# Final rows of the first 128 tokens moved from VectorE to ScalarE and accumulating transfers, and VectorE's last operations written in a fixed order

## The chip, the core and the metric

The program runs on one NeuronCore of a Trainium2 chip. Its engines are TensorE (PE in the rows, its weight load PEld), VectorE (DVE), ScalarE (ACT), GpSimd (POOL) and SyncE (SP); SP, ACT and POOL can issue transfers, which 16 DMA engines carry out. The metric is the device time of one execution in microseconds, lower being better.

## What is computed

One decoder layer in fp32 for 512 tokens of width 2048. An input projection feeds differential attention, a Mamba-2 mixer and cross-attention; their gated outputs are put side by side (`mixed`, 512 x 2048) and go through the output projection, a norm and the residual. Only the end matters here:

```python
def rms_norm(x, w):
    y = x * lax.rsqrt(jnp.mean(x * x, axis=-1, keepdims=True) + NORM_EPS)
    return y * w
...
    mixed = jnp.concatenate([diff_out, ssd_out, xattn_out], axis=-1)
    return x + rms_norm(mixed @ w_out, post_norm_w)
```

The norm needs the sum of squares over all 2048 columns of a token before any of its columns can be written.

## The kernel before

**Output projection.** `mixed @ w_out` is made in four groups `g` of 512 columns. In each, seven block products `q` of 256 columns take the place of eight, and their sums give the result. A product has four units `u`, and each number is split into a high and a low part, so each small product is three matmuls of 128x256 (lines 99 to 101). The sums are gathered in SBUF tiles `oacc{g}{c}`: 128 tokens by `t` (2) by `r` (2) by 256 columns, `c` being the half of the 512 tokens. A "row" `t` in the code below is one block of 128 tokens: rows 0 and 1 lie in `c` = 0, rows 2 and 3 in `c` = 1.

**The tail.** In the last group the products 5 and 3 touch only `c` = 1, and they are made last, for row 2 (PSUM tiles `oq35`, `oq33`) and then for row 3 (`oq35b`, `oq33b`). Rows 0 and 1 are complete before. For each row, in `write_rows`:

1. ScalarE has squared the sums (`finish`, line 1066; tile `jk`, results in `ssq`), VectorE has multiplied them by the norm's weight and by -0.5 or 0.5 (line 1070).
2. VectorE adds the eight partial sums of `ssq` (line 1082), ScalarE takes the logarithm and the exponential (lines 291, 292), and VectorE sharpens the root in three tiny operations (lines 293 to 295). The result `ors` is -2 times the reciprocal root.
3. VectorE makes `xr = oacc * ors + xr` for four pieces of 512 columns (line 1088). `xr{t}{h}` is the row of `x`, loaded in two halves of 512 KB by SP (line 1078) into eight buffers that the weights of the projection leave free.
4. SP stores the row in two halves (line 1096); row 3 goes in four pieces of 256 KB, alternately by SP and ScalarE's queue (line 1093).

**Order.** A scheduler with a timeline of its own orders the instructions of each engine. `tc.keep_in_program_order(op)` fixes one to its place in the text, and `tc.issue_after(x)` keeps what is inside behind `x`. In before, nothing that VectorE does in the tail is fixed. POOL issues the accumulating loads of weights (line 968, pieces `oA`, 512 KB each in runs of 1 KB), the last of them at 851.28 us, and has nothing after it.

Of the kernel before, what the change touches and what calls it, by code (L numbers as in the profile page):

```python
# [15 lines left out]
AF = mybir.ActivationFunctionType  # L16
ALU = mybir.AluOpType
AX = mybir.AxisListType
PSUM = bass.MemoryType.PSUM

P = 128
# [3 lines left out]
NT = S // P  # L25
M = 256
EPS = 1e-6
# [42 lines left out]
def hymba_kernel(ctx: ExitStack, tc: tile.TileContext, x, mem, positions, pre_norm_w, w_in,  # L70
# [3 lines left out]
    nc = tc.nc  # L74
    x2, mem2, out2 = x[0], mem[0], out[0]
# [4 lines left out]
    small = ctx.enter_context(tc.tile_pool(name="small", bufs=4))  # L80
# [5 lines left out]
    def bank(tag, name):  # L86
        if tag == "d":
            return psd.tile([P, 512], F32, tag="d", name=name)
        return pss.tile([P, 512], F32, tag=tag, name=name, bufs=SIDE[tag])

    def ft(pool, shape, tag, name, bufs=None, dt=F32):
        kw = {} if bufs is None else {"bufs": bufs}
        return pool.tile(shape, dt, tag=tag, name=name, **kw)
# [54 lines left out]
    epsc = const.tile([P, 1], F32, name="epsc")  # L148
# [140 lines left out]
    def neg2_rstd(y, t, v):  # L289

        nc.scalar.activation(t, v, AF.Ln, bias=epsc)
        nc.scalar.activation(y, t, AF.Exp, scale=-0.5)
        nc.vector.tensor_tensor(t, y, y, ALU.mult)
        nc.vector.scalar_tensor_tensor(t, v, EPS, t, ALU.add, ALU.mult)
        nc.vector.scalar_tensor_tensor(y, t, 3.0, y, ALU.subtract, ALU.mult)
# [3 lines left out]
    def push(name, side="right"):  # L299
        cm = tc.tile_pool(name=name, bufs=1, side=side, reuse_waits="tile")  # L300
        open_pools.append(cm)
        return cm.__enter__()
# [7 lines left out]
    def slot(n, name, dt=F32):  # L310

        if n % 2 == 0:
            slot_pairs[n // 2] = slots_p.tile([P, 2, S], dt, tag=f"s{n // 2}", name=name)
        return slot_pairs[n // 2][:, n % 2]
# [63 lines left out]
    ps = dense_xs(memT, [bank("d", f"mv{t}") for t in range(2)], 512)  # L378
# [17 lines left out]
    for t in range(NT):  # L396
        rs = row_rstd(x_rows[t], f"x{t}")
# [12 lines left out]
    for h in range(4):  # L410
        ps = dense_ws(memT, M, f"mk{h}")
# [29 lines left out]
    ps = dense_xs(hT, [bank("dddt"[t].replace("t", "tr"), f"v0_{t}") for t in range(NT)], 264)  # L441
# [37 lines left out]
    for c in range(2):  # L479
        for i in range(2):  # L480
            h = 2 * c + i
            ps = dense_ws(hT, S, f"xq{h}")
# [6 lines left out]
            for qp in range(2):  # L489
# [11 lines left out]
                for j in range(2):  # L501
                    nc.scalar.activation(pt[:, j], sc[:, j * M:(j + 1) * M], AF.Exp,
                                         bias=nm[:, j:j + 1], scale=XSC, accum_out=ls[:, j:j + 1])
# [16 lines left out]
            o = slot(12 + h, f"xo{h}")  # L520
# [123 lines left out]
    for g in range(2):  # L644
        for i in range(2):
            ps = dense_ws(hT, S, f"z{g}{i}")
# [15 lines left out]
        rt = ft(sp, [P, S], "rt", f"rt{g}", 1)  # L662
# [47 lines left out]
    for t in range(NT):  # L710
        for b in range(4):
            src = slice(32 * t, 32 * t + 32)
            dst = slice(32 * b, 32 * b + 32)
            ts = slice(t * P, (t + 1) * P)
# [18 lines left out]
    for c in range(2):  # L733
        for i in range(2):
            ps = dense_ws(hT, S, f"xg{c}{i}")
# [163 lines left out]
    for p in range(4):  # L899
        if p:  # L900
            vb = [bank("d", f"v{p}_{t}") for t in range(2)]
            ps = dense_xs(hT, [vb[t // 2][:, t % 2 * 256:t % 2 * 256 + 256] for t in range(NT)],
                          256, share=2)
            v_pair[p] = evac_v(ps, str(p))
        q = [rope(dense_ws(hT, S, f"q{2 * p + i}"), "q", 2 * p + i) for i in range(2)]
        k = [rope(dense_ws(hT, S, f"k{2 * p + i}"), "k", 2 * p + i) for i in range(2)]
# [20 lines left out]
    op = push("op")  # L927
# [13 lines left out]
    ssq = const.tile([P, NT, 8], F32, name="ssq")  # L941
# [4 lines left out]
    NG = D // 512  # L946
# [106 lines left out]
    oacc = {}  # L1053

    def acc(g, r, c):

        if (g, c) not in oacc:
            oacc[g, c] = slots_p.tile([P, 2, 2, 256], F32, tag=f"s{2 * g + c}",
                                      name=f"oacc{g}{c}")
        return oacc[g, c][:, :, r]  # L1060

    def finish(g, r, c, ts=(0, 1)):
        o = acc(g, r, c)
        jk = ft(ep, [P, 256], "jk", f"jk{g}{r}{c}{ts[0]}", 2, BF16)
        for t in ts:
            nc.scalar.activation(jk, o[:, t], AF.Square, scale=1.0 / math.sqrt(D),
                                 accum_out=ssq[:, 2 * c + t, 2 * g + r:2 * g + r + 1])
        w = pws[g][:, r].unsqueeze(1).broadcast_to([P, len(ts), 256])
        tt = slice(ts[0], ts[-1] + 1)
        nc.vector.scalar_tensor_tensor(o[:, tt], o[:, tt], (-0.5, 0.5)[r], w, ALU.mult,  # L1070
                                       ALU.mult)

    xr = {}

    def load_rows(t):
        for h in range(2):
            xr[t, h] = raw_tile(f"xr{t}{h}")
            nc.sync.dma_start(xr[t, h], x2[t * P:(t + 1) * P, h * 1024:(h + 1) * 1024])

    def write_rows(t):  # L1080
        ss = ft(small, [P, 1], "ss", f"oss{t}")
        nc.vector.tensor_reduce(ss, ssq[:, t], AX.X, ALU.add)
        y = ft(small, [P, 1], "rs", f"ors{t}")
        tt = ft(small, [P, 1], "rt", f"ort{t}")
        neg2_rstd(y, tt, ss)
        for g in range(NG):
            xs = xr[t, g // 2][:, (g % 2) * 512:(g % 2) * 512 + 512]
            nc.vector.scalar_tensor_tensor(
                xs, oacc[g, t // 2][:, t % 2].rearrange("p r c -> p (r c)"), y, xs,
                ALU.mult, ALU.add)  # L1090
            q = nc.scalar if t == NT - 1 and g % 2 else nc.sync
            if t == NT - 1:
                q.dma_start(out2[t * P:(t + 1) * P, 512 * g:512 * g + 512],
                            xr[t, g // 2][:, (g % 2) * 512:(g % 2) * 512 + 512])
            elif g % 2:
                q.dma_start(out2[t * P:(t + 1) * P, 512 * g - 512:512 * g + 512], xr[t, g // 2])

    def product(n, ps, ts=(0, 1)):
        hi, lo = split[n]
        g, q, u = seq[n]  # L1100
        for t in ts:
            tsl = slice(t * P, (t + 1) * P)
            for kk in range(2):
                bh, bl = comb[2 * u + kk][PROD[q][1]]
                last = mm3(ps[:, t], bh[:, tsl], bl[:, tsl], hi[kk], lo[kk],
                    u == 0 and kk == 0 and t == ts[0], u == 3 and kk == 1 and t == ts[-1])
        return last
# [28 lines left out]
    qps, qps2 = {}, {}  # L1136
    for n, (g, q, u) in enumerate(seq):
# [13 lines left out]
        ps = qps[g, q]  # L1151
        if n < len(seq) - 8:
            last = product(n, ps)
# [4 lines left out]
        T = lambda o, x, y: V.tensor_tensor(o, x, y, ALU.add)  # L1158
# [14 lines left out]
        if q == 3:  # L1173
# [2 lines left out]
            T(acc(g, 0, 1), acc(g, 0, 1), ps)  # L1176
            finish(g, 1, 1)
            finish(g, 0, 1)
    for t in (0, 1):
        load_rows(t)  # L1180
        write_rows(t)
    g = NG - 1
    N = len(seq)
    for t in (0, 1):
        load_rows(2 + t)
        for q, n in ((5, N - 8), (3, N - 4)):
            ps = qps2[q] if t else qps[g, q]
            with tc.issue_after(last.ins):
              for u in range(4):
                last = product(n + u, ps, (t,))  # L1190
            for r in range(2):
                if q == 5 or r == 0:
                    T(acc(g, r, 1)[:, t], acc(g, r, 1)[:, t], ps[:, t])
            finish(g, int(q == 5), 1, (t,))
        write_rows(2 + t)
    while open_pools:
        pop()

# [32 lines left out]
```

## Time and profile before

| | us |
|---|---|
| median of three runs | 904.86 |
| those runs | 901.61, 904.86, 905.66 |
| the profiled execution, its time | 903.45 |
| its span, first to last instruction | 901.7 |
| last matmul on the chain of waits starts | 890.72 |
| last operation of VectorE ends | 898.24 |

Times in the rows count from the span's start. The profiled execution is 1.75 us longer than its span, and lies 1.41 us under the median of the three runs, inside their spread.

### The profile page before, as it was taken

What the parts mean: (1) busy time and instruction counts of PE and PEld (TensorE: products, weight loads), DVE (VectorE), ACT (ScalarE), POOL (GpSimd) and SP (SyncE); (2) the same over time, 40 slices, a digit from 0 to 9 for tenths busy, and PEclk for the clock granted to TensorE, in tenths of its full rate; (3) what the DMA queues carried; (4) which work ended last, traced back from release to release, by engine and by line L of the source; (5) the groups of instructions that cost most, each with busy time, mean ns of one, the idle gap of its engine ahead of it and who ended that gap; (6) DMA issues with size and microseconds to landing.
All of it is one profiled execution on the core that took longest, in us unless ns stands there. A gap on an engine that the chain in (4) does not pass through costs nothing.

```text
span 901.7 us, 13703 instructions
## 1 busy us (share of the span) xinstructions
PE 882.7 (98%) x5187; PEld 773.9 (86%) x5187; DVE 607.6 (67%) x1150; ACT 467.9 (52%) x823; POOL 131.2 (15%) x139
## 2 busy tenths in 40 slices
PE   8999999999999999999999999999999999999995
PEld 6899888888888888898889889888888888999995
DVE  5775545595565542485768578676877689877797
ACT  4754234455356643344455445456676675564562
POOL 3310000006000212330230123023100011110200
PEclk9999999999999999999999999999999999999998
DMA  9862322354343333433342433334232475785946
GB/s 307 302 166 71 94 71 71 102 143 115 95 130 81 94 94 93 116 98 92 95 117 71 106 95 82 94 97 115 71 94 74 126 191 120 181 195 119 214 131 245
DMA packets 150205, 111.86 MB, mean 124 GB/s; under 512 B 8869, under 2 KB 139634, under 8 KB 150138
## 3 DMA queue, kind: packets, MB, share of 16 engines
q1 hardware_dynamic: 141434, 102.58, 40.1%
q0 software_dynamic: 8416, 7.87, 5.7%
q8 instruction: 41, 0.67, 0.3%
q10 hardware_dynamic: 288, 0.52, 0.2%
q14 instruction: 26, 0.21, 0.1%
HBM read 102.02 MB, written 4.21 MB: 118 GB/s over the span
## 4 chain that ended last, share of the span: by engine, by line
PE 87%; DVE 4%; DMA 4%; issue 3%; ACT 1%; POOL 0%; SPq 0%; DVEq 0%; POOLq 0%; ACTq 0%
PE v L101 3%; PE v L99 3%; PE v L100 3%; PE q L99 3%; PE q L100 3%; PE k L100 3%; PE k L99 3%; PE q L101 3%; PE xbc L99 3%; PE k L101 3%; PE xbc L101 3%; PE xbc L100 3%; PE oq L100 3%; PE dg L101 3%; PE dg L100 3%; DMA oA<-in_w_out_dram 3%
## 5 line engine op out<-in xcount | busy, mean ns | idle before, releaser
L104 DVE TENSOR_TENSOR wlo<-raw,whi 128x1024 fp32r<-128x1024 f32 (+2 forms) x121 | 152.1, 1257 | 119.4 <-ACT whi L247 105.8
L247 ACT ACTIVATE whi<-raw 128x1024 fp32r<-128x1024 f32 (+1 forms) x104 | 110.2, 1060 | 127.4 <-issue 36.7
L1048 ACT ACTIVATE owh<-oA 128x512 fp32r<-128x512 f32 x106 | 65.8, 630 | 59.2 <-PE oq L101 46.1
L104 DVE TENSOR_TENSOR owl<-oA,owh 128x512 fp32r<-128x512 f32 x106 | 71.6, 690 | 16.5 <-ACT owh L1048 16.1
L100 PE MATMUL v<-wlo,hT 128*128 128x256 f32 (+1 forms) x256 | 72.9, 285 | 0.0
L101 PE MATMUL v<-whi,hT 128*128 128x256 f32 (+1 forms) x256 | 72.6, 285 | 0.0
L99 PE MATMUL v<-whi,hT 128*128 128x256 f32 (+1 forms) x256 | 72.4, 285 | 0.0
L803 ACT ACTIVATE p<-sc,nm 128x128 f32<-128x128 f32 (+3 forms) x64 | 33.4, 525 | 60.0 <-DVE nm L799 52.8
L100 PE MATMUL k<-hT,whi 128*128 128x512 f32 x128 | 51.0, 398 | 0.0
L101 PE MATMUL xbc<-hT,wlo 128*128 128x512 f32 x128 | 50.8, 397 | 0.0
L100 PE MATMUL dg<-hT,whi 128*128 128x512 f32 x128 | 50.7, 396 | 0.0
L101 PE MATMUL dg<-hT,wlo 128*128 128x512 f32 x128 | 50.7, 396 | 0.0
L99 PE MATMUL q<-hT,whi 128*128 128x512 f32 x128 | 50.7, 396 | 0.0
L100 PE MATMUL xbc<-hT,whi 128*128 128x512 f32 x128 | 50.6, 395 | 0.0
L99 PE MATMUL dg<-hT,whi 128*128 128x512 f32 x128 | 50.5, 395 | 0.0
L101 PE MATMUL k<-hT,wlo 128*128 128x512 f32 x128 | 50.5, 395 | 0.0
L100 PE MATMUL q<-hT,whi 128*128 128x512 f32 x128 | 50.4, 394 | 0.0
L99 PE MATMUL k<-hT,whi 128*128 128x512 f32 x128 | 50.4, 394 | 0.0
L99 PE MATMUL xbc<-hT,whi 128*128 128x512 f32 x128 | 50.4, 394 | 0.0
L101 PE MATMUL q<-hT,wlo 128*128 128x512 f32 x128 | 50.3, 393 | 0.0
L100 PEld LDWEIGHTS v<-wlo,hT 128*128 128x128 f32 x256 | 48.5, 189 | 0.3
L99 PEld LDWEIGHTS v<-whi,hT 128*128 128x128 f32 x256 | 48.3, 189 | 0.3
(445 smaller groups left out, 2569.0 us busy)
## 6 DMA issues: line engine op xcount, KB each, us to landing
raw<-in_w_in_dram SPq DMA_DIRECT2D x104, 512.0 KB, 3.9
oA<-in_w_out_dram SPq DMA_DIRECT2D x32, 512.0 KB, 5.5
raw<-in_w_mem_kv_dram SPq DMA_DIRECT2D x15, 512.0 KB, 5.4
oA<-in_w_out_dram POOLq DMA_DIRECT2D x14, 512.0 KB, 6.9
x_rows<-in_x_dram SPq DMA_DIRECT2D x8, 512.0 KB, 8.8
xr<-in_x_dram SPq DMA_DIRECT2D x8, 512.0 KB, 7.9
out_dram<-xr SPq DMA_DIRECT2D x6, 512.0 KB, 2.7
mem_rows<-in_mem_dram SPq DMA_DIRECT2D x8, 256.0 KB, 5.8
```

The costliest lines, as they stand in the source:

```text
L99: nc.tensor.matmul(ps, ah, bh, start=start, stop=False)
L100: nc.tensor.matmul(ps, ah, bl, start=False, stop=False)
L101: return nc.tensor.matmul(ps, al, bh, start=False, stop=stop)
L104: nc.vector.tensor_tensor(lo, src, hi.bitcast(F32), ALU.subtract)
L247: nc.scalar.activation(hi[:, :n], raw[:, :n], AF.Copy)
L803: nc.scalar.activation(pc[c][:, :w], sc[c][:, :w], AF.Exp, bias=nm[:, c:c + 1], scale=DSC, accum_out=ls[:, c:c + 1])
L1048: nc.scalar.activation(hi, src, AF.Copy)
```

## The change

For row 0, VectorE's four operations of step 3 are gone. ScalarE multiplies the sums by `ors` in place (line 1209, four copies of 128x512 with a scale), and POOL's queue adds each result onto `xr` in SBUF by an accumulating transfer of 256 KB (line 1210). The two stores of row 0 go by POOL's queue as well, behind the accumulations (line 1221), instead of SP's. Rows 1 to 3 keep their operations on VectorE, but those are now written out by hand among the last additions, weighings and roots, and fixed in that order. The loads of `x` are asked for earlier in the text.

```diff
-        nc.vector.scalar_tensor_tensor(o[:, tt], o[:, tt], (-0.5, 0.5)[r], w, ALU.mult,
-                                       ALU.mult)
+        op = nc.vector.scalar_tensor_tensor(o[:, tt], o[:, tt], (-0.5, 0.5)[r], w, ALU.mult,
+                                            ALU.mult)
+        if len(ts) == 1:
+            tc.keep_in_program_order(op)
...
-    def write_rows(t):
...
+    pin = tc.keep_in_program_order
...
+    def row_sum(t):
+        ys[t] = [ft(small, [P, 1], k, f"o{k}{t}") for k in ("ss", "rs", "rt")]
+        pin(nc.vector.tensor_reduce(ys[t][0], ssq[:, t], AX.X, ALU.add))
+        v, y, r = ys[t]
+        nc.scalar.activation(r, v, AF.Ln, bias=epsc)
+        nc.scalar.activation(y, r, AF.Exp, scale=-0.5)
+
+    def root(t):
+        v, y, r = ys[t]
+        pin(nc.vector.tensor_tensor(r, y, y, ALU.mult))
+        pin(nc.vector.scalar_tensor_tensor(r, v, EPS, r, ALU.add, ALU.mult))
+        pin(nc.vector.scalar_tensor_tensor(y, r, 3.0, y, ALU.subtract, ALU.mult))
+
+    def add_last(t, q):
+        ps = qps2[q] if t == 3 else qps[g, q]
+        for r in ((1, 0) if q == 5 else (0,)):
+            pin(T(acc(g, r, 1)[:, t - 2], acc(g, r, 1)[:, t - 2], ps[:, t - 2]))
+        squares(g, int(q == 5), 1, (t - 2,))
+
+    def rows_out(t, gs):
+        for b in gs:
+            o = oacc[b, t // 2][:, t % 2].rearrange("p r c -> p (r c)")
+            x = xr[t, b // 2]
+            xs = x[:, (b % 2) * 512:(b % 2) * 512 + 512]
+            if t == 0:
+                nc.scalar.activation(o, o, AF.Copy, scale=ys[t][1])
+                nc.gpsimd.dma_start(xs, o, accum_op=ALU.add)
+            else:
+                pin(nc.vector.scalar_tensor_tensor(xs, o, ys[t][1], xs, ALU.mult, ALU.add))
...
+    def first_rows_out():
+        for h in range(2):
+            nc.gpsimd.dma_start(out2[:P, 1024 * h:1024 * h + 1024], xr[0, h])
...
+    row_sum(0)
+    row_sum(1)
+    add_last(2, 5)
+    root(0)
+    root(1)
+    rows_out(0, range(NG))
+    first_rows_out()
+    rows_out(1, (0,))
+    weigh(g, 1, 1, (0,))
+    rows_out(1, (1,))
+    add_last(2, 3)
+    rows_out(1, (2,))
+    row_sum(2)
+    weigh(g, 0, 1, (0,))
+    rows_out(1, (3,))
+    root(2)
+    add_last(3, 5)
+    rows_out(2, (0,))
+    weigh(g, 1, 1, (1,))
+    rows_out(2, (1, 2))
+    add_last(3, 3)
+    rows_out(2, (3,))
+    row_sum(3)
+    weigh(g, 0, 1, (1,))
+    root(3)
+    rows_out(3, range(NG))
```

`squares` and `weigh` are the two halves of the old `finish`. TensorE's instructions are the same in the same order, and SP's loads too.

VectorE, from the additions of row 2's product 5 (`oq35`) on, in the program before; the digit after `ors` is the row:

```order
L1158 TENSOR_TENSOR oacc31_8598<-oacc31_8598,oq35_8745 128x256 x2
L295 SCALAR_TENSOR_TENSOR ors0_8767<-ort0_8768,ors0_8767 128x1
L293 TENSOR_TENSOR ort1_8787<-ors1_8786 128x1
L1088 SCALAR_TENSOR_TENSOR xr00_8761<-oacc00_6884,ors0_8767,xr00_8761 128x512
L1088 SCALAR_TENSOR_TENSOR xr00_8761<-oacc10_7449,ors0_8767,xr00_8761 128x512
L1088 SCALAR_TENSOR_TENSOR xr01_8763<-oacc20_7956,ors0_8767,xr01_8763 128x512
L1088 SCALAR_TENSOR_TENSOR xr01_8763<-oacc30_8463,ors0_8767,xr01_8763 128x512
L294 SCALAR_TENSOR_TENSOR ort1_8787<-oss1_8784,ort1_8787 128x1
```

The same place now:

```order
+L1149 TENSOR_TENSOR oacc31_8598<-oacc31_8598,oq35_8745 128x256 x2
+L1193 TENSOR_TENSOR ort0_8875<-ors0_8874 128x1
+L1194 SCALAR_TENSOR_TENSOR ort0_8875<-oss0_8873,ort0_8875 128x1
+L1195 SCALAR_TENSOR_TENSOR ors0_8874<-ort0_8875,ors0_8874 128x1
+L1193 TENSOR_TENSOR ort1_8881<-ors1_8880 128x1
+L1194 SCALAR_TENSOR_TENSOR ort1_8881<-oss1_8879,ort1_8881 128x1
+L1195 SCALAR_TENSOR_TENSOR ors1_8880<-ort1_8881,ors1_8880 128x1
+L1212 SCALAR_TENSOR_TENSOR xr10_8765<-oacc00_6884,ors1_8880,xr10_8765 128x512
+L1073 SCALAR_TENSOR_TENSOR oacc31_8598<-oacc31_8598,pw3_8461 128x256
+L1212 SCALAR_TENSOR_TENSOR xr10_8765<-oacc10_7449,ors1_8880,xr10_8765 128x512
```

The four operations on `xr00` and `xr01` are gone, and the first on `xr10` stands right behind the two roots; in before, the four of row 0 stood ahead of it.

POOL at the end of its program (its last loads of weights are the two rows without a sign):

```order
 L968 DMA oA11_30_8028<-in_w_out_dram 128x4x256
 L968 DMA oA11_31_8030<-in_w_out_dram 128x4x256
-L1227 UNCONDITIONAL_BRANCH
-L1227 ISA
+L1210 DMA xr00_8761<-oacc00_6884 128x512
+L1210 DMA xr00_8761<-oacc10_7449 128x512
+L1210 DMA xr01_8763<-oacc20_7956 128x512
+L1210 DMA xr01_8763<-oacc30_8463 128x512
+L1221 DMA out_0_dram<-xr00_8761 128x1024
+L1221 DMA out_0_dram<-xr01_8763 128x1024
```

Four accumulations and two stores stand one behind the other on a queue that was empty here.

SP's loads of `x` and stores of rows 0 and 1, as they are now and were before:

```order
+L1087 DMA xr31_8775<-in_x_dram 128x1024
+L1087 DMA xr10_8765<-in_x_dram 128x1024
+L1218 DMA out_0_dram<-xr10_8765 128x1024
+L1218 DMA out_0_dram<-xr11_8767 128x1024
+L1218 DMA out_0_dram<-xr20_8769 128x1024
```

`xr10` is the last of the eight loads, in both programs; the stores of `xr00` and `xr01`, which stood between it and that of `xr10`, have left SP's queue.

## Rows read from the trace of the kernel before

**Rows 1.** The page, its first part: busy time of each engine.

```profile
PE 882.7 (98%) x5187; PEld 773.9 (86%) x5187; DVE 607.6 (67%) x1150; ACT 467.9 (52%) x823; POOL 131.2 (15%) x139
```

**Rows 2.** The chain of waits, 890 to 902 us: start, length, what.

```profile
890.72 0.13 PE oq33b L101
...
892.37 2.65 DVE xr L1088 x4
...
895.50 0.75 DVE xr L1088
...
896.92 1.32 DVE xr L1088 x2
```

**Rows 3.** Timeline of VectorE: start, length, line, operation, tiles, forms, count, [idle before].

```profile
882.29 0.75 DVE L1158 TENSOR_TENSOR oacc<-oacc,oq 128x256 f32<-128x256 f32 x2
...
883.14 2.74 DVE L1088 SCALAR_TENSOR_TENSOR xr<-oacc,ors,xr 128x512 f32<-128x512 f32 x4
...
886.72 2.74 DVE L1088 SCALAR_TENSOR_TENSOR xr<-oacc,ors,xr 128x512 f32<-128x512 f32 x4
...
894.93 0.15 DVE L293 TENSOR_TENSOR ort<-ors 128x1 f32<-128x1 f32 x1
895.12 0.16 DVE L294 SCALAR_TENSOR_TENSOR ort<-oss,ort 128x1 f32<-128x1 f32 x1
...
895.50 2.74 DVE L1088 SCALAR_TENSOR_TENSOR xr<-oacc,ors,xr 128x512 f32<-128x512 f32 x4
```

**Rows 4.** Timeline of ScalarE in the tail.

```profile
882.34 0.20 ACT L292 ACTIVATE ors<-ort 128x1 f32<-128x1 f32 x1
...
891.33 0.42 ACT L1066 ACTIVATE jk<-oacc 128x256 bf16<-128x256 f32 x1 [0.25 <-DVE oacc L1158]
...
892.40 0.29 ACT L291 ACTIVATE ort<-oss,epsc 128x1 f32<-128x1 f32 x1 [0.57 <-DVE oss L1082]
892.73 0.20 ACT L292 ACTIVATE ors<-ort 128x1 f32<-128x1 f32 x1
896.95 1.66 ACTq L1093 DMA_DIRECT2D out_dram<-xr  x2
```

**Rows 5.** Timeline of ScalarE: three copies of 128x512 back to back.

```profile
858.34 1.66 ACT L1048 ACTIVATE owh<-oA 128x512 fp32r<-128x512 f32 x3
```

**Rows 6.** Windows; the last three columns are clock, DMA share of 16 engines, GB/s.

```profile
884.00:885.00 1.00, 1.00 (x11) 1.00 (x10) 1.00 (x2) 0.00 (x0) 0.00 (x0) 1.00 0.05 20
886.00:888.00 2.00, 2.00 (x19) 2.00 (x18) 1.97 (x5) 0.51 (x2) 0.00 (x0) 1.00 0.97 393
...
892.00:894.00 2.00, 0.00 (x0) 0.00 (x0) 2.00 (x5) 0.50 (x2) 0.00 (x0) 0.98 0.02 8
895.00:900.00 5.00, 0.00 (x0) 0.00 (x0) 3.14 (x8) 0.00 (x0) 0.00 (x0) 0.50 0.99 380
900.00:902.00 2.00, 0.00 (x0) 0.00 (x0) 0.00 (x0) 0.00 (x0) 0.00 (x0) 0.50 0.01 3
```

**Rows 7.** Windows around the last two accumulating loads of POOL's queue.

```profile
846.00:848.00 2.00, 2.00 (x19) 2.00 (x18) 1.80 (x3) 1.14 (x4) 0.00 (x0) 1.00 1.09 375
...
850.00:851.00 1.00, 1.00 (x11) 1.00 (x10) 0.98 (x2) 0.88 (x4) 0.00 (x0) 1.00 0.48 69
851.00:856.00 5.00, 4.71 (x40) 4.50 (x39) 1.69 (x3) 1.56 (x4) 1.28 (x1) 1.00 1.18 180
```

**Rows 8.** Timeline of POOL, and line 968's 14 transfers, issue to landing.

```profile
848.48 1.28 POOL L968 DMA_DIRECT2D oA<-in_w_out_dram  x1 [8.71 <-DVE owl L104]
...
DMA to landing us min/median/max: 5.8/6.9/9.7
```

**Rows 9.** POOL's smallest transfers, 32 rows of 512 bytes: duration of an issue in ns.

```profile
L715 POOL DMA_DIRECT2D cosT<-ang x16: 496/498/498, 217.1 to 226.0; - x16
```

**Rows 10.** The last two loads of `x` on SP: the last one's issue, the one before's landing.

```profile
878.15 0.33 SPq L1078 DMA_DIRECT2D xr<-in_x_dram  x1
...
xr<-in_x_dram SPq DMA_DIRECT2D x1, 512.0 KB, 8.0
```

More of the change, by code (lines that the diff above doesn't have):

```diff
@@ L1060, in acc, with squares @@
         return oacc[g, c][:, :, r]
-    def finish(g, r, c, ts=(0, 1)):
+    def squares(g, r, c, ts=(0, 1)):
         o = acc(g, r, c)
@@ L1067, in finish, with weigh @@
                                  accum_out=ssq[:, 2 * c + t, 2 * g + r:2 * g + r + 1])
+    def weigh(g, r, c, ts=(0, 1)):
+        o = acc(g, r, c)
         w = pws[g][:, r].unsqueeze(1).broadcast_to([P, len(ts), 256])
         tt = slice(ts[0], ts[-1] + 1)
-        nc.vector.scalar_tensor_tensor(o[:, tt], o[:, tt], (-0.5, 0.5)[r], w, ALU.mult,
-                                       ALU.mult)
+        op = nc.vector.scalar_tensor_tensor(o[:, tt], o[:, tt], (-0.5, 0.5)[r], w, ALU.mult,
+                                            ALU.mult)
+        if len(ts) == 1:
+            tc.keep_in_program_order(op)
+    def finish(g, r, c):
+        squares(g, r, c)
+        weigh(g, r, c)
     xr = {}
@@ L1078, in load_rows @@
             nc.sync.dma_start(xr[t, h], x2[t * P:(t + 1) * P, h * 1024:(h + 1) * 1024])
-    def write_rows(t):
[L1081 to L1096, printed above, removed]
     def product(n, ps, ts=(0, 1)):
@@ L1178, in hymba_kernel @@
             finish(g, 0, 1)
-    for t in (0, 1):
-        load_rows(t)
-        write_rows(t)
+    pin = tc.keep_in_program_order
     g = NG - 1
     N = len(seq)
+    for t in range(NT):
+        load_rows(t)
     for t in (0, 1):
-        load_rows(2 + t)
         for q, n in ((5, N - 8), (3, N - 4)):
@@ L1188, in hymba_kernel @@
             with tc.issue_after(last.ins):
[L1189 to L1195, printed above, removed]
+                for u in range(4):
+                    last = product(n + u, ps, (t,))
+    ys = {}
+    def row_sum(t):
[4 more added lines that the diff above has]
+        nc.scalar.activation(y, r, AF.Exp, scale=-0.5)
@@ new lines, in rows_out @@
+    def rows_out(t, gs):
[8 more added lines that the diff above has]
+                pin(nc.vector.scalar_tensor_tensor(xs, o, ys[t][1], xs, ALU.mult, ALU.add))
+            dst = out2[t * P:(t + 1) * P]
+            if t == NT - 1:
+                q = nc.scalar if b % 2 else nc.sync
+                q.dma_start(dst[:, 512 * b:512 * b + 512], xs)
+            elif b % 2 and t:
+                nc.sync.dma_start(dst[:, 512 * b - 512:512 * b + 512], x)
```

## The prediction

> **What bounds the kernel now.** I read the page's busy shares first: TensorE is busy 98% of the span [rows 1], and its instructions don't change, so only what lies behind the last matmul can move. The chain of waits shows that stretch: the last matmul on it starts at 890.72, and from there VectorE holds the end, with four operations of 128x512 for row 2 (892.37), three tiny ones for row 3's root, and four for row 3 from 895.50 [rows 2]. VectorE's timeline says why row 2 comes so late: it works without a break from 882.29 on, row 0 taking 2.74 us from 883.14 and row 1 as much from 886.72 [rows 3]. Last come the windows, for what the chain doesn't name. The DMA engines carry 380 GB/s at a share of 0.99 from 895 to 900 and next to nothing from 900 on; from 892 to 894 they idle (0.02) [rows 6]. So the last 2 MB of stores run at what these engines can move, after a gap in which VectorE had nothing for them. Two things hold the tail, VectorE's queue and then the transfers.
>
> **VectorE.** Four operations leave it. Four back to back take 2.74 us with one duration of 0.75 [rows 3], so one costs (2.74 - 0.75) / 3 = 0.66, and 2.66 us leave. The same group's 2 additions of 128x256 in 0.75 give 0.34 each, and a root's tiny operations start 0.19 apart. The new order, worked through: additions of row 2 end at 882.29 + 0.68 = 882.97, six tiny operations at 884.1. ScalarE's exponential for row 1 ended at 882.54 [rows 4], so they don't wait. Then comes the first operation on `xr10`, the last load of `x`. It was issued at 878.15; the load before it took 8.0 us [rows 10], and between 884 and 885, before any store moves data, packets are still seen at 20 GB/s [rows 6]. So some load lands after 884, and this is the last in the queue; I take 885.3. The near end is no wait at all, the far end its neighbour's 8.0 us again, 886.2. Before, this wait was covered by row 0, which stood ahead; now nothing covers it, and since the order is fixed, the additions, weighings and roots of rows 2 and 3 queue behind it.
>
> From there to the last operation stand twelve of 128x512 (8.0), eight of 128x256 (2.7), two roots (1.15), two sums of squares (0.3) and a wait of some 0.4 for row 3's square, logarithm and exponential (0.42, 0.29 and 0.20 [rows 4]), which one operation on row 2 and a weighing partly cover: 12.55 us. Started at 885.4, the last ends at 897.95; before, at 898.24. A start at 884.1 would give 896.65, one at 886.3 would give 898.85. Thus of 2.66 us taken off VectorE 0.3 reach its end; 1.3 are lost to `xr10`, the rest to roots that no longer stand between long operations.
>
> **ScalarE.** Its four copies cost nothing on the path: three of that size take 1.66 us, about 0.52 apart [rows 5], so from row 0's root at 883.5 they run to 885.8, and what stands behind them, row 2's next square, needs an addition that VectorE makes after 887. If that addition came at 885, the square would be late by 0.8 us, which row 1's operations would still cover.
>
> **Transfers.** Here the change adds. Stores stay 4.19 MB (four rows of 1.05 MB); four accumulations of 262 KB are new. Their price: a 1 KB packet of an accumulating load takes an engine 1.18 x 16 x 5 us over 879 packets (180 GB/s for 5 us) = 107 ns, a plain one 1.09 x 16 x 2 / 732 = 48 ns [rows 7], a plain one of 4 KB 0.97 x 16 x 2 / 192 = 162 ns [rows 6]. So plain packets cost 10 ns and 38 per KB, and accumulation adds 59 to 1 KB. Packets here are of 2 KB; no row has those. If the extra is per packet they take 145 ns, if per KB 204; with packets overlapping as the share of 1.18 shows, eight per engine take 0.98 to 1.38 us, four transfers 3.9 to 5.5. I take 4.6, between the two, as a source in SBUF instead of HBM is nearer to neither. If they cost what a plain transfer costs, it would be 2.8 (1.05 MB at 380 GB/s). Stores: rows 0 to 2 at 393, row 3 at 380 GB/s [rows 6], 8.0 + 2.8 = 10.8.
>
> When does this begin? The first copy ends at 884.3. POOL's issue lasts 0.50 us for 32 rows [rows 9] and 1.28 for 512 runs [rows 8]; this one has 128. Data of the issue at 848.48 shows only from 850 to 851 on [rows 7, 8], some 2 us later; with the shorter issue I take 1.6, so 884.6 + 1.6 = 886.2. Row 1's first store is issued at 887.1. If the engines don't idle from 886.2, data ends at 886.2 + 4.6 + 10.8 = 901.6; before it ended at 900.0. That is +1.6. With 5.5 for the accumulations and a start at 886.6 it is +2.9; at plain prices -0.2. Do they idle? Each two accumulations must land before POOL issues a store of row 0, but meanwhile rows 1 and 2 keep them busy, so I add nothing.
>
> The Trainium skill ("DMA: Bandwidth & Descriptors", section "Issuing engines are not separate DMA queues") says that transfers from any engine's queue run on the same 16 DMA engines, so that another queue brings no bandwidth. The trace agrees as far as it goes: share 0.99 with two queues storing and no more than 380 GB/s. The same page ("Anatomy of one DMA — SWDGE (gpsimd) path") puts a transfer from GpSimd at 2.0 us plus its bytes at 436 GB/s; an estimate from it, 2.4 us for all accumulations, would end the data at 899.4. This case's accumulating loads of 512 KB land after 5.8 us at least, not the 3.2 of that fit, so the measured rate decides.
>
> **The sum.** The later of the two bounds counts: VectorE gives -0.3, the transfers +1.6. The profiled execution took 903.45 (span 901.7 and 1.75 around it), so 905.0. It lies 1.4 under the median of the runs and 0.5 under the mean of all four times (903.9), so 905.0 is what I forecast for the median too; 0.5% of the time, 4.5 us, is about what a measurement can tell from no change.
>
> **Rivals.**
> - *VectorE's time reaches the end.* `xr10` lands by 884.1 and accumulations cost no more than plain transfers: VectorE ends 1.6 earlier, data 0.2 earlier, or up to 1.6 if the accumulations also begin before 885. For it: between 884 and 885 a share of 0.05 is left, about one engine of 16 [rows 6]. Against it: 107 ns against 48 for packets of one size. 901.9 to 903.2; I price it at 902.5.
> - *POOL's queue ends last.* Its six transfers stand in line, and the second store waits for the fourth accumulation. With POOL's issues 0.7 to 1.28 us apart, that one goes out between 886.7 and 888.4. Should it land over 9 us later, the store is issued at 897.5, its data starts some 2 us behind that and takes 1.3, past the 900.0 at which data ends now: this is the point from which POOL decides. For it: 9.7 us was seen, and here row 1's and row 2's stores, 1.33 us per half, stand between. Against it: 6.9 is the median, for transfers twice as large [rows 8]. At 9.7 it gives +1.8; with one or two such halves in between +3.1 to +4.5, which is 906.6 to 908.
>
> **How the numbers follow.** I give the transfers' bound 0.55, VectorE's gain 0.27, POOL's queue 0.18. The gain can't pass 4.5 us, as 2.66 us is all that leaves VectorE, and of POOL's cases only the worst does; what is left for both sides is the spread of the runs, 4 us among three. Faster 0.04, same 0.89, slower 0.07. The likeliest case alone spans 903.2 to 906.8; with most of the gain's and of POOL's cases the range is 901.5 to 908.0.
>
> **What would show it.** Right: no operation of VectorE on row 0 of `xr`, VectorE's first idle stretch ahead of row 1 ended by a load of `x` near 885.3, its last operation near 898, a DMA share near 1 or above from 887 to 901, accumulations landing 4 us or more after issue. Wrong: idle DMA engines between 890 and 896, or VectorE's row 3 starting by 894 and the span under 901: then accumulations are cheap. A last landing on POOL's queue, with SP and ScalarE done, would be the second rival.

## The result, and the profile after

The changed kernel takes 907.81 us (median of nine runs, 907.03 to 909.36); the kernel before takes 902.77 over its nine runs beside them (901.61 to 905.66); later runs of it on other chips gave 902.9 to 903.1. The ratio is 1.0051, with a 95% interval from 1.0042 to 1.0060: 5.0 us slower by the medians, 3.8 to 5.4 by the interval, which is clear of no change. The profiled executions lie nearer together (907.03 and 903.45, spans 905.3 and 901.7), because the one after is the lowest of its nine and the one before is above its median. Steps are compared below in these two, sizes in the medians.

The page's first part, after:

```profile
PE 883.5 (98%) x5187; PEld 774.5 (86%) x5187; DVE 605.5 (67%) x1146; ACT 470.6 (52%) x827; POOL 135.9 (15%) x145
```

TensorE is what it was [rows 1], and by the timeline its last matmul starts at 890.32 (890.55 before; the chain in [rows 2] counts from 890.72). VectorE has lost its four operations, ScalarE has gained four and POOL six transfers. The chain of waits from there on (start, length, what):

```profile
877.88 7.60 DMA xr<-in_x_dram
...
885.58 0.75 DVE xr L1212
...
891.52 1.32 DVE xr L1212 x2
...
895.09 0.75 DVE xr L1212
...
896.50 1.32 DVE xr L1212 x2
```

It begins with a load of `x`, goes through VectorE as in [rows 2], and stops at 897.82 while the span goes on to 905.3: what fills those 7.5 us it does not name. VectorE's timeline, for [rows 3]:

```profile
883.57 0.16 DVE L1195 SCALAR_TENSOR_TENSOR ors<-ort,ors 128x1 f32<-128x1 f32 x1
885.58 0.75 DVE L1212 SCALAR_TENSOR_TENSOR xr<-oacc,ors,xr 128x512 f32<-128x512 f32 x1 [1.86 <-DMA xr<-in_x_dram]
...
894.50 0.16 DVE L1193 TENSOR_TENSOR ort<-ors 128x1 f32<-128x1 f32 x1 [0.26 <-ACT ors L1189]
...
895.09 2.74 DVE L1212 SCALAR_TENSOR_TENSOR xr<-oacc,ors,xr 128x512 f32<-128x512 f32 x4
```

It waits 1.86 us for the load, then works through and ends at 897.83, 0.4 sooner than before. ScalarE's and POOL's part of the timeline:

```profile
883.30 2.56 ACT L1209 ACTIVATE oacc<-oacc,ors 128x512 f32<-128x512 f32 x4 [0.28 <-DVE ors L1195]
```

```profile
884.32 0.89 POOL L1210 DMA_DIRECT2D xr<-oacc  x1 [31.92 <-ACT oacc L1209]
885.46 2.64 POOL L1210 DMA_DIRECT2D xr<-oacc  x3 [0.25 <-ACT oacc L1209]
890.48 0.56 POOL L1221 DMA_DIRECT2D out_dram<-xr  x1 [2.39 <-DMA xr<-oacc]
896.18 0.54 POOL L1221 DMA_DIRECT2D out_dram<-xr  x1 [5.14 <-issue]
```

Four accumulations are issued by 888.1, and row 0's two stores wait for them, each for two; the second store goes out at 896.18, 5.1 us after the first one's issue ended. The two lines' transfers, from issue to landing (the semaphore update that tells of a transfer's end):

```profile
L1210 POOL DMA_DIRECT2D xr<-oacc x4: 870/1034/1522, 884.3 to 886.6; - x4
...
DMA to landing us min/median/max: 3.3/5.6/9.0
```

```profile
L1221 POOL DMA_DIRECT2D out_dram<-xr x2: 537/550/563, 890.5 to 896.2; - x2
...
DMA to landing us min/median/max: 6.2/6.6/7.1
```

The windows, in the stretches of [rows 6] and one more (the last three columns are clock, DMA share, GB/s):

```profile
884.00:885.00 1.00, 1.00 (x11) 1.00 (x10) 0.00 (x0) 1.00 (x3) 0.68 (x1) 1.00 0.06 25
886.00:888.00 2.00, 2.00 (x19) 2.00 (x18) 2.00 (x5) 0.30 (x1) 2.00 (x3) 1.00 1.04 172
892.00:894.00 2.00, 0.00 (x0) 0.00 (x0) 2.00 (x6) 0.57 (x3) 0.00 (x0) 1.00 1.05 304
895.00:900.00 5.00, 0.00 (x0) 0.00 (x0) 2.79 (x5) 0.00 (x0) 0.54 (x1) 0.50 1.02 395
900.00:902.00 2.00, 0.00 (x0) 0.00 (x0) 0.00 (x0) 0.00 (x0) 0.00 (x0) 0.50 1.02 382
902.00:904.00 2.00, 0.00 (x0) 0.00 (x0) 0.00 (x0) 0.00 (x0) 0.00 (x0) 0.50 0.11 41
```

This is what the chain leaves out. From 886 to 902 no window of 2 us has a share under 1.01, so the DMA engines are full: the gap that [rows 6] show from 892 to 894 (share 0.02) is filled (1.05), and they still carry 382 GB/s from 900 to 902, where before they carried 3. Between 886 and 888 they are just as busy but move 172 GB/s instead of 393: they accumulate. The trace's packets from 885.6 on, summed and divided by 16 engines:

```
                        queue      packets      median ns   us of 16 engines
after, accumulations    POOL's     512 x 2 KB      189         6.21
after, row 0's stores   POOL's     256 x 4 KB      165         2.65
after, all stores       SP's, ACT's                            8.2
after, everything       885.78 to 903.21                      17.20
before, everything      885.60 to 900.22                      10.53
```

17.2 us of work in 17.4 us of time. One more thing shows only in the last line of the program, where each queue is brought to rest. First after, then before:

```profile
L1281 POOLq EVENT_SEMAPHORE  x4: 17/17/17, 904.6 to 905.2; - x4
L1281 POOLq DRAIN  x3: 46/98/8371, 896.2 to 905.0; - x3
L1281 SPq DRAIN  x3: 7/7/7, 903.8 to 904.8; - x3
```

```profile
L1227 POOLq EVENT_SEMAPHORE  x4: 17/17/17, 901.0 to 901.6; - x4
L1227 POOLq DRAIN  x3: 46/93/7920, 851.3 to 901.5; - x3
L1227 SPq DRAIN  x3: 7/7/13, 900.9 to 901.2; - x3
```

SP reaches its end at 903.8, but POOL's long drain, begun at 896.16, lasts 8.37 us, to 904.53, which is 2.2 us past the landing of POOL's last store (896.2 + 6.2 = 902.4); the closing steps of the other engines follow. Before, the same drain began at 851.3 and was over by 859.2. So POOL holds the end by some 0.7 us.

### The profile page after: what moved, and what is told of

It is laid out like the page before. It is cut to its first block, busy times and chain, and to the rows that moved or that the text cites. A ratio compares the mean times of both kernels' runs of the same rounds, so it can differ in the third digit from the quotient of the medians.

```text
span 905.3 us, 13711 instructions
## 1 busy us (share of the span) xinstructions
PE 883.5 (98%) x5187; PEld 774.5 (86%) x5187; DVE 605.5 (67%) x1146; ACT 470.6 (52%) x827; POOL 135.9 (15%) x145
## 4 chain that ended last, share of the span: by engine, by line
PE 87%; DVE 4%; DMA 4%; issue 2%; ACT 1%; SPq 0%; POOL 0%; DVEq 0%; POOLq 0%; ACTq 0%
PE oq L100 4%; PE v L101 3%; PE oq L101 3%; PE v L99 3%; PE v L100 3%; PE q L99 3%; PE q L100 3%; PE oq L99 3%; PE k L100 3%; PE k L99 3%; PE xbc L99 3%; PE q L101 3%; PE k L101 3%; PE xbc L100 3%; PE xbc L101 3%; PE dg L99 3%
```

## The experiments

Each run is given by its median, by its ratio to the runs of the kernel before on the same chip, and, since the last matmul comes up to 1.3 us sooner or later from one execution to another, by two times of the profiled execution that count from that matmul's start: to the end of the last DMA packet ("data") and to the end of the span ("tail"). The expectations that speak of theory A mean the full DMA engines; theories B and C are named in each. Two kernels, the one without accumulation and the one with plain copies, leave the addition of `x` to row 0 out.

```
kernel                                    median   ratio (95%)             data    tail
before                                    902.77                            9.7   11.15
after                                     907.81   1.0051 (1.0042, 1.0060) 12.9   14.98
no accumulation, pieces stored directly   901.39   0.9979 (0.9969, 0.9988)  7.9    9.51
row 0's stores on SP                      906.88   1.0038 (1.0025, 1.0050) 12.9   14.18
fixed order only                          904.25   1.0013 (1.0004, 1.0022) 10.1   11.54
GpSimd adds instead of transfers          905.17   1.0025 (1.0016, 1.0034) 11.9   13.42
x loads reordered                         907.83   1.0052 (1.0039, 1.0065) 12.9   16.21
... and two accumulations instead of 4    903.38   1.0008 (0.9999, 1.0017) 10.2   11.55
... and accumulated in the output         903.78   1.0009 (1.0000, 1.0017) 10.3   11.79
before, last store on POOL                906.16   1.0036 (1.0023, 1.0048) 10.0   13.26
plain copies instead of accumulations     903.21   1.0007 (0.9998, 1.0015) 10.3   11.68
offload without the fixed order           906.96   1.0049 (1.0037, 1.0061) 12.8   14.80
free order, two pieces into the output    903.02   0.9999 (0.9991, 1.0008) 10.0   11.47
free order, three pieces into the output  903.36   1.0004 (0.9995, 1.0013)  9.8   11.31
```

The four kernels that accumulate four pieces into SBUF and then store row 0 end their data 12.8 to 12.9 us after the last matmul, whichever queue stores row 0, whatever order VectorE has and whether it waits for `x`; before ends it at 9.7. What follows the data is 1.5 us before, 2.1 after, and 3.3 where a store of POOL's is last by far. So of the 3.8 us between the two tails 3.2 are later data and 0.6 the end of the program.

**No accumulation.** ScalarE's pieces of row 0 are stored as they are, so that the addition of `x` is left out for row 0.

```diff
-                nc.gpsimd.dma_start(xs, o, accum_op=ALU.add)
+                nc.gpsimd.dma_start(out2[:P, 512 * b:512 * b + 512], o)
-    first_rows_out()
```

Expected: 

> Left out: the residual x of row 0; ScalarE's four scaled pieces are stored as they are by GpSimd's queue (four plain stores of 256 KB) in place of four accumulating transfers and two stores. Theory A (the accumulations fill the DMA engines, 6 us of all 16 at 189 ns a packet): VectorE's last operation stays at 897.8, the data ends near 900.0 as in the kernel before, span 900.8 to 901.8, ratio to before 0.998 to 1.001, so all of the +5 us is gone. Theory B (GpSimd's queue, its second store and its drain, ends last): the same, as its queue is empty by 890. Theory C (the fixed order of VectorE costs the time): still slower than before, ratio 1.003 or more.

Measured: 901.39, 6.4 us under the changed kernel and 1.7 under the kernel before. Nothing waits for row 0's `x` here, the last load of `x` is issued at 875.63 instead of 877.88, and VectorE has no wait ahead of row 1 either; its last operation ends at 895.86, which the expectation had missed, and the span of 899.7 is shorter than it said. What the change costs lies in the accumulations and what they bring with them (the stores that wait for them, and POOL's queue), and without them taking row 0 off VectorE does pay.

**Row 0's stores on SP.**

```diff
-            nc.gpsimd.dma_start(out2[:P, 1024 * h:1024 * h + 1024], xr[0, h])
+        nc.sync.dma_start(out2[:P, 1024 * h:1024 * h + 1024], xr[0, h])
```

The two issues stand in the text behind the operations of rows 1 and 2, so that SP's queue isn't held up early.

Expected: 

> The accumulating transfers stay, the two stores of row 0 go by SP's queue instead of GpSimd's, behind row 1's and among row 2's. Theory A (the engines are full): the same bytes at the same price, data ends within 0.7 us of the changed kernel's 903.2; GpSimd's drain, which follows its last landing by about 2 us, ends near 898 and no longer holds the end, so span 904 to 905, ratio to before 1.003 to 1.005. Theory B (GpSimd's queue sets the end): 2 us from issue to data and 2.2 of drain are gone, span 902.3 or less, ratio 1.001 or less.

Measured: 906.88, 0.9 less than the changed kernel, with intervals that overlap, and still 3.8 above before. POOL's stores and the drain behind them are at most the small part of the loss. SP's second store of row 0 waited for the fourth accumulation until 896.45 and held up row 2's last store behind it, yet the data ended as long after the last matmul as in the changed kernel. The Trainium skill ("DMA: Bandwidth & Descriptors", section "Issuing engines are not separate DMA queues") says that every queue ends in the same 16 DMA engines; this run agrees, its windows from 888 to 902 show shares of 1.01 to 1.10 with another queue storing.

**Fixed order only.** Row 0 goes back to VectorE and SP; VectorE's order stays that of the change.

```diff
-            if t == 0:
-                nc.scalar.activation(o, o, AF.Copy, scale=ys[t][1])
-                nc.gpsimd.dma_start(xs, o, accum_op=ALU.add)
-            else:
-                pin(nc.vector.scalar_tensor_tensor(xs, o, ys[t][1], xs, ALU.mult, ALU.add))
+            pin(nc.vector.scalar_tensor_tensor(xs, o, ys[t][1], xs, ALU.mult, ALU.add))
```

Expected: 

> Only the fixed order of VectorE: row 0's four operations are back on VectorE, in the place where the changed kernel gives them to ScalarE, and its stores on SP's queue. Theory A or B: no accumulations and nothing on GpSimd, so the +5 us is gone; VectorE covers its wait for x with row 0 (2.66 us from 883.8) and ends row 3 at 898.3 to 899.0 against 898.24 before, span 901.7 to 902.6, ratio 1.000 to 1.002. Theory C (the order costs it): ratio 1.004 or more.

Measured: 904.25, 1.1 above before (0.4 to 2.0). VectorE's last operation ends 8.19 us after the last matmul's start, 7.69 before. The order costs something, not the 5 us.

**GpSimd adds.** The additions become operations of POOL's engine, and SP stores row 0.

```diff
-                nc.gpsimd.dma_start(xs, o, accum_op=ALU.add)
+                nc.gpsimd.tensor_tensor(xs, xs, o, ALU.add)
```

Expected: 

> As the changed kernel, but GpSimd itself adds ScalarE's pieces to x (four operations of 128x512, 1.3 us each as its other such operations take, up to 2.4) in place of the accumulating transfers, and SP stores row 0. Theory A: no added bytes, data ends by 900.0, span 901 to 901.7, ratio 0.998 to 1.000. Theory B: the same, as GpSimd issues no transfer. Against both: VectorE's operations with two inputs in SBUF slow beside GpSimd's; then those of row 1 take over 0.75 us each and VectorE's end moves past 898.5, ratio 1.001 to 1.004.

Measured: 905.17, 2.0 above before. The DMA engines are no longer full (share 0.00 from 886 to 888), but VectorE's timeline shows a new price, the one that the end of the expectation weighed; POOL's row first, then VectorE's:

```profile
885.41 6.13 POOL L1210 TENSOR_TENSOR xr<-xr,oacc 128x512 f32<-128x512 f32 x4 [31.57 <-ACT oacc L1209]
```

```profile
887.17 1.51 DVE L1073 SCALAR_TENSOR_TENSOR oacc<-oacc,pw 128x256 f32<-128x256 f32 x1
888.60 1.78 DVE L1212 SCALAR_TENSOR_TENSOR xr<-oacc,ors,xr 128x512 f32<-128x512 f32 x1
...
892.42 0.73 DVE L1212 SCALAR_TENSOR_TENSOR xr<-oacc,ors,xr 128x512 f32<-128x512 f32 x1
```

While POOL adds (885.4 to 891.5), VectorE's operations take 1.78 instead of 0.75 us and 1.51 instead of 0.42, and fall back to 0.73 once POOL is done; an addition that reads one of its two tiles from PSUM, at 890.31, took 0.41 all the same. VectorE ends at 901.6, so this loss has another cause than the change's.

**`x` loads reordered.** The buffer that comes free last goes to row 3.

```diff
-    for t in range(NT):
-        load_rows(t)
+    for t, h in ((0, 0), (0, 1), (3, 1), (1, 0), (1, 1), (2, 0), (2, 1), (3, 0)):
+        xr[t, h] = raw_tile(f"xr{t}{h}")
+        nc.sync.dma_start(xr[t, h], x2[t * P:(t + 1) * P, h * 1024:(h + 1) * 1024])
```

Expected: 

> The changed kernel with one difference: the buffer that comes free last goes to the second half of row 3's x instead of the first half of row 1's, so that row 1's first operation has nothing to wait for. Theory A (the DMA engines are full from the first accumulation to the end, so that VectorE's time is worth nothing): VectorE's idle 1.86 us goes and its last operation ends near 895.9 instead of 897.83, but the time stays within 0.7 us of the changed kernel's, 4.2 to 5.2 us above the kernel before. Theory B (the late x load holds up VectorE and with it the last stores): about 1.9 us less than the changed kernel, 2.5 to 3.3 us above the kernel before.

Measured: 907.83, what the changed kernel takes. VectorE's row 1 starts at 883.52 without a wait and its last operation ends at 895.76, 2.1 us sooner than after (1.8 counted from the last matmul); nothing of it arrives. Row 1's stores come sooner, the accumulations beside them later (to 895.9 instead of 894.7), and the engines have the same work. The end of this kernel is a plainer case of what after shows in part. POOL's timeline, then the last line:

```profile
890.94 0.56 POOL L1222 DMA_DIRECT2D out_dram<-xr  x1 [3.09 <-DMA xr<-oacc]
896.94 0.54 POOL L1222 DMA_DIRECT2D out_dram<-xr  x1 [5.44 <-issue]
```

```profile
L1282 POOLq EVENT_SEMAPHORE  x4: 17/17/17, 905.5 to 906.2; - x4
L1282 POOLq DRAIN  x3: 46/97/8573, 896.9 to 906.0; - x3
L1282 SPq DRAIN  x3: 7/7/7, 903.7 to 905.8; - x3
```

SP's and ScalarE's last packets end at 901.7 (903.2 in after), so the stores of row 3 did gain; but POOL's second store, behind the fourth accumulation, ends at 903.0, and POOL's drain only at 905.5. Once VectorE is sooner, POOL's queue ends the program alone.

**Two accumulations instead of four.** On top of the reordered loads, pieces 0 and 1 of row 0 stay with VectorE and SP.

```diff
-            if t == 0:
+            if t == 0 and b > 1:
...
-        for h in range(2):
-            nc.gpsimd.dma_start(out2[:P, 1024 * h:1024 * h + 1024], xr[0, h])
+        nc.gpsimd.dma_start(out2[:P, 1024:], xr[0, 1])
```

Expected: 

> As the kernel with the x loads reordered, but only the last two pieces of row 0 go by ScalarE, accumulation and POOL's store; the first two are VectorE's again, in the time that it had stood idle, and their store is SP's. Theory A: two accumulations fewer take about 3 us of the engines' time away (half of the 6 measured) and POOL's one store lands long before the end; VectorE ends near 897.2, an estimate from 895.9 and two operations of 0.67; the transfers end just behind it, and the time is 0.2 to 1.1 us under the kernel before. Theory B, in which only VectorE counts and the accumulations do not: the time follows VectorE, which has 1.3 us more than in the kernel with the loads reordered, so it would be slower than that kernel by about 1.3 us.

Measured: 903.38, 4.5 under the kernel with four, but 0.4 above before (-0.1 to 1.5) instead of under it. The accumulations take 2.97 us of the engines instead of 6.18, as expected, and VectorE ends 6.9 us after the last matmul's start. What was missed is the end of the transfers: the accumulations, with SP's stores between them, end only at 893.2, POOL's store goes out at 894.35, and the data ends at 901.3.

**Accumulated in the output.** Row 0's `x` goes from DRAM into the output (issued at 867.7, landed at 875.1), and ScalarE's pieces are added there. The loads of `x` are reordered here too.

```diff
-                nc.gpsimd.dma_start(xs, o, accum_op=ALU.add)
+                nc.gpsimd.dma_start(out2[:P, 512 * b:512 * b + 512], o, accum_op=ALU.add)
...
+            pin(nc.sync.dma_start(out2[:P], x2[:P]))
```

Expected: 

> As the kernel with the x loads reordered, but row 0's x goes from DRAM straight into the output near 869 us, where the DMA engines are not full, and the four accumulations add ScalarE's pieces to the output, so that row 0 has no store behind them (2.7 us of the engines' time less, and nothing waits for the last accumulation). Theory A: 2.7 to 3.5 us less than the changed kernel, 1.0 to 2.0 us above the kernel before, if an accumulation into DRAM takes the engines as long as one into SBUF (189 ns a packet of 2 KB); how long it does is read from its packets. Theory B: as the kernel with the loads reordered, since VectorE's work is the same.

Measured: 903.78, 4.0 under the changed kernel, 0.8 above before (0.0 to 1.5), somewhat less than the 1.0 to 2.0 expected. The accumulations into DRAM take 178 ns a packet of 2 KB (6.36 us of the engines), so they cost what those into SBUF do. What is gained is put down to row 0's stores and POOL's late end, which are gone; no run parts the two. VectorE's last operation ends 5.7 us after the last matmul's start, the data 10.3 after it: the transfers bind.

**Before, with its last store on POOL's queue.**

```diff
-            q = nc.scalar if t == NT - 1 and g % 2 else nc.sync
+            q = (nc.gpsimd if g == 3 else nc.scalar) if t == NT - 1 and g % 2 else nc.sync
```

Expected: 

> The kernel before with one store moved: the last 256 KB of row 3 leave by POOL's queue instead of ScalarE's. It prices that queue at the end of a program. Theory: data start about 2.3 us behind the issue, and POOL's drain ends about 2 us behind the last landing (both as in the changed kernel), so the time is 1.5 to 4 us above the kernel before. Rival: what POOL's queue takes at the end is no more than another queue takes: within 0.5 us.

Measured: 906.16, 3.2 above before (2.1 to 4.3), for one moved store of 256 KB. In the profile it is 2.1 us, by tails, of which later data is 0.3; the data started 1.2 us behind the issue, not the 2.3 expected. Its last packet ends at 899.7; the last line shows why the span goes to 903.0:

```profile
L1227 POOLq EVENT_SEMAPHORE  x4: 17/17/17, 902.3 to 902.9; - x4
L1227 POOLq DRAIN  x3: 46/98/4528, 897.7 to 902.8; - x3
L1227 SPq DRAIN  x3: 7/7/7, 900.9 to 902.5; - x3
```

SP is at its end 1.2 us after the last packet, POOL's drain 2.5 after it (897.7 + 4.5 = 902.2).

**Plain copies.** The transfers of the change stay, with their sizes, queue and waits, and copy where they added; the addition of `x` is left out for row 0.

```diff
-                nc.gpsimd.dma_start(xs, o, accum_op=ALU.add)
+                nc.gpsimd.dma_start(xs, o)
```

Expected: 

> The changed kernel with its four transfers of row 0's pieces as plain copies instead of additions; it leaves out the addition of x to row 0. Sizes, queue, waits and stores stay. Theory A (an accumulation takes the DMA engines about twice as long as a copy): the packets of 2 KB take near 90 ns instead of 189, the four take about 3 us of the engines' time less, and the time is 0.5 to 2.5 us above the kernel before instead of 4.9. Rival (the price is the further 1 MB through the engines and POOL's slow queue, whatever the transfers do): within 1 us of the changed kernel, 4 to 6 us above the kernel before.

Measured: 903.21, 4.6 under the changed kernel and 0.3 above before (-0.2 to 1.4), a little under the 0.5 to 2.5 expected. Windows of 8 us, the changed kernel first, then this one:

```profile
886.00:894.00 8.00, 4.60 (x39) 4.40 (x37) 7.93 (x21) 2.09 (x9) 2.66 (x4) 1.00 1.07 247
894.00:902.00 8.00, 0.00 (x0) 0.00 (x0) 3.46 (x8) 0.44 (x2) 0.54 (x1) 0.55 1.02 395
```

```profile
886.00:894.00 8.00, 4.10 (x35) 3.89 (x33) 7.56 (x22) 2.02 (x8) 1.70 (x4) 1.00 1.01 385
894.00:902.00 8.00, 0.00 (x0) 0.00 (x0) 1.58 (x3) 0.00 (x0) 0.00 (x0) 0.52 0.62 237
```

The engines are equally full from 886 to 894, but move 385 instead of 247 GB/s, and are done sooner. The packets from 885.6 on come to 13.1 us of 16 engines instead of 17.2. The copies run as packets of 4 KB in 172 ns, 86 per 2 KB against the accumulations' 189; row 3's plain stores, in packets of 2 KB, take 84, so the larger packet is not what makes them cheap; a transfer takes 3.8 us to land in the median instead of 5.6. VectorE also has no wait for `x` here, which the reordered loads showed to be worth nothing while the accumulations stay. A kernel with plain copies and the wait was not run; but the last store of row 3 is issued at 895.61 and the data ends 4.5 us later (1.9 in before), so here too VectorE was ahead of the transfers.

**Offload without the fixed order.** `write_rows` of the kernel before, with row 0 as in the change.

```diff
+            if t == 0:
+                nc.scalar.activation(o, o, AF.Copy, scale=y)
+                nc.gpsimd.dma_start(xs, o, accum_op=ALU.add)
+                continue
```

Expected: 

> The kernel before with row 0 by ScalarE, accumulations and POOL's stores, but with VectorE's operations in the scheduler's order, as before. Theory A: row 0's copies start some 0.7 us sooner after the last sums than in the fixed order, and otherwise nothing changes, since the DMA engines are full from there on: 3.5 to 5 us above the kernel before. Rival (the fixed order makes the loss): within 1.2 us of the kernel before.

Measured: 906.96, 4.0 above before, 0.9 under the changed kernel. The rival that the order makes the loss falls. Whether the order's 1 us is in those 0.9 isn't shown: the two intervals lie almost on each other.

**Candidates: free order, two or three pieces added to the output.**

```diff
+            if t == 0 and g >= FIRST:
+                o = oacc[g, 0][:, 0].rearrange("p r c -> p (r c)")
+                nc.scalar.activation(o, o, AF.Copy, scale=y)
+                nc.gpsimd.dma_start(out2[:P, 512 * g:512 * g + 512], o, accum_op=ALU.add)
+                continue
```

`FIRST` is 2 or 1; the loads are reordered, and `x` of these columns goes from DRAM to the output ahead of the tail.

Expected with two: 

> A candidate: the kernel before, VectorE's operations in the scheduler's order; the second half of row 0's x goes from DRAM into the output near 869 us, and pieces 2 and 3 of row 0 are scaled by ScalarE and added to the output by accumulating transfers; pieces 0 and 1 stay VectorE's; x loads as in the reordered kernel. Theory A: the accumulations' 3 us of the engines lie in the 5 us before the last matmul, where the engines are not full before, and VectorE ends 1.2 to 1.4 us sooner; 0.3 to 1.2 us under the kernel before. Theory A is wrong on the cover if it is slower than the kernel before.

Expected with three: 

> As that candidate with three pieces of row 0 accumulated and one with VectorE, its store a piece of its own. Theory A: 1.5 us more of the engines' time and 0.67 us less of VectorE's; where the transfers bind it is 0.3 to 1.2 us slower than the candidate with two, where VectorE binds it is up to 0.7 us faster.

Measured: 903.02 and 903.36, no change that can be told from the kernel before. The gain expected of two is missed, and the third piece changes nothing that is clear of noise. VectorE's timeline with two pieces says why:

```profile
893.12 0.42 DVE L1070 SCALAR_TENSOR_TENSOR oacc<-oacc,pw 128x256 f32<-128x256 f32 x1 [0.57 <-ACT jk L1066]
...
894.21 0.16 DVE L293 TENSOR_TENSOR ort<-ors 128x1 f32<-128x1 f32 x1 [0.60 <-ACT ors L292]
...
894.80 2.74 DVE L1094 SCALAR_TENSOR_TENSOR xr<-oacc,ors,xr 128x512 f32<-128x512 f32 x4
```

VectorE ends 7.7 us after the last matmul's start, as in the kernel before: in the scheduler's order the time freed from row 0 comes back as waits for ScalarE, 0.57 and 0.60 us, in the chain of row 3. In before, row 2's four operations stood there and covered them. The fixed order splits row 2's operations around that chain: with row 0 off VectorE and no wait for `x`, it ends 5.7 after the last matmul, where the offload in the scheduler's order ended 7.9 after it. Two pieces into the output in the fixed order were not tried.

## Why the prediction was right, and where its size was off

The mechanism held: VectorE's gain does not reach the end, the transfers do, and the kernel becomes slower. The size did not: the sum gave +1.6, the profiled pair +3.6, the medians +5.0, past the likeliest case's own range (906.8) and 0.2 us inside the upper end of the whole range. That end came from the cases of POOL's queue, not from the case that the forecast rests on; that the range held is in part luck. By the line of 4.5 us that the prediction drew, 5.0 is a slowdown, to which it gave 0.07; the interval, 3.8 to 5.4, lies on both sides of that line.

- **What bounds it.** As read: TensorE unchanged, the tail VectorE's and then the transfers'. [rows 6] showed the idle 892 to 894 that the change fills.
- **VectorE.** Row 1's first operation was forecast for 885.4 after a wait for `xr10` until 885.3; it came at 885.58, and the last operation ended at 897.83 for 897.95. The reordered loads give VectorE these 2 us back and leave the time where it was, so this term is worth nothing either way as long as the accumulations stand.
- **ScalarE.** The copies, forecast from 883.5 to 885.8, ran from 883.30 to 885.86 and held nobody up.
- **Transfers.** Start, stores and "the engines don't idle" held: first packet at 885.78 (886.2), stores 10.8 us as summed, shares of 1.01 to 1.09 from 886 to 902. The term that was mis-sized is "I take 4.6" for the accumulations, between 3.9 and 5.5: they took 6.21 us of the engines. A packet took 189 ns, inside the 145 to 204 of the estimate. The error is mostly the step behind it, the division by the share of 1.18 [rows 7]: with stores mixed in, the share was at most 1.09, and over the whole stretch 17.20 us of packets took 17.43 us of time, so nothing was given back. Without that division the estimate's middle, 175 ns, is 5.6 us, and 189 ns by 32 packets an engine 6.05. The division is 1.0 us of the miss, the dearer packet 0.5.
- **Plain or accumulating.** That the extra is in the addition, which the estimate took from two rows of other sizes, is shown by the plain copies: 4.6 us between kernels that differ in it (and in a wait that was worth nothing where it could be tried by itself).
- **The sum.** It let the end follow the last data as before. SP did follow, from 903.2 to 903.8, but POOL's drain lasted to 904.5. The two, 1.4 us of later data (903.2 for 901.6, less the 0.2 by which before's data ended later than read) and 0.7 of drain, make 905.0 into 907.1, and 907.03 was taken. No step of the prediction had the drain. That the median of the changed kernel lies 0.8 above its profiled execution, and that of before 0.7 under its own, makes the rest of the 5.0. The order costs some 1 us in the medians (0.4 to 2.0) and hardly shows in the profiled tails (0.4); which part of the rest is due to it and which is spread stays open.
- **VectorE's time reaches the end.** Wrong for this change, as weighed: accumulations do not cost what plain transfers cost. Even with its condition met it brought no gain: the plain copies, with no wait for `x`, took 0.3 more than before, where the rival had 0.95 less (902.5 against 903.45). Only with no second transfer at all was VectorE's time worth something, 1.7 us.
- **POOL's queue ends last.** Half right. Its sum was off: the point of 9 us was held against 900.0, where data ended before, and not against the 901.6 of the prediction's own sum, and 9.7 us gives by its steps +1.5, not +1.8. The deciding point, over 9 us from issue to landing for the fourth accumulation, was met to the row (9.0), the second store went out at 896.18 instead of 897.5, and it landed at 902.4, ahead of the last store of row 3. By landings POOL was not the last; by its drain it was, by 0.7 us, and with the loads reordered it was the last by far. The rival's price, 906.6 to 908, holds the measured time, though most of that time is the transfers'. The two cases should not have been held apart: DMA engines full of accumulations make both.
- **Its signs.** All but one came: the first accumulation landed after 3.3 us, not 4 or more; the median was 5.6.

## What to carry to other kernels

Ask of an accumulating transfer what the DMA engines have left in that very stretch: here it moved data at less than half the rate of a copy, its bytes come on top of the store that waits for it, and here 2.7 us of VectorE were bought with 6.2 us of engines that were full afterwards to the end. Time taken off an engine counts only where nothing full stands between it and the end; before an operation is moved, look which resource is idle there, and for how long. In these runs POOL's queue was the wrong one for the last transfers: its drain ended 2.0 to 2.2 us behind its last landing, and the end of the program waited for it.

## What the runs showed of the hardware that was not expected

- An accumulating packet of 2 KB held a DMA engine for 189 ns into SBUF and 178 into DRAM; a plain copy of 4 KB between the same tiles took 172.
- POOL's drain at the end of the program ended 2.4 to 2.6 us behind the last packet of its queue in every kernel here that used that queue in the tail; one store of 256 KB moved to it cost 3.2 us (2.1 to 4.3).
- Beside POOL's additions VectorE's operations with two tiles from SBUF took up to 3.6 times as long (1.51 for 0.42 us), and POOL needed 1.53 us for an addition of 128x512.
- Issuing an accumulation took POOL 0.87 to 1.52 us, a plain transfer of the same size 0.54.
